# Giving every large SBUF slot of a transformer-block kernel a size that is a whole number of 256 bytes

## The chip, the cores and the metric

The kernel runs on one core of one Trainium2 chip. The metric is the device time of one execution in microseconds. The kernel before takes 2279.22 us (median of 3 runs, 2278.37 to 2279.22).

## What is computed

One layer of an encoder block on x, 1024 rows (T) of 1024 channels (D), all in float32:

```
x <- x + 1/2 * SwiGLU_1(RMSNorm(x))            (D_FF = 2816)
h  = RMSNorm(x);  [x_m | z_m | x_r | y_r] = h @ W_in
y_m = mLSTM head group (4 heads of 256 channels, causal)
y_r = RG-LRU channel group (4 block-diagonal gate groups of 256, conv of 4, scan)
x <- x + concat[RMSNorm(y_m), RMSNorm(y_r)] @ W_out
x <- x + 1/2 * SwiGLU_2(RMSNorm(x))
out = RMSNorm_final(x)
```

Nearly all the arithmetic is matrix products with 1024 rows: two feed-forward blocks (1024 to 2 x 2816 to 1024), the input projection (1024 to 4096), the output projection (2048 to 1024), and the attention-like products of the four mLSTM heads.

## The kernel before

**Products.** The channels lie on the 128 partitions, the rows of x along the free axis. A float32 operand is carried as two float32r parts, hi and lo, and a product is the sum of three passes, hi*hi + hi*lo + lo*hi (`PASSES`). So each step of 128 channels issues three matmuls, each with a weight load of 128x128 of its own and with 512 columns streamed. `project_half` (L275 to L280, matmul on L278) makes a 128x512 tile of an up or input projection: 24 matmuls, 8 steps of channels (k) by 3 passes. The stationary operand is `wu`, a weight tile with its hi part and, 4096 bytes on, its lo part; the streamed operand is `hT`. `products` (L284 to L299, matmul on L295) makes the down and output projections the same way, with `wu` stationary and a pair of hi and lo activations (`u8` in the feed-forward blocks, other tiles in the output projection) streamed.

**Stages.** `ffn` (L311) makes two tiles of the hidden layer (192 matmuls on L278), then the 96 matmuls on L295 that add two earlier ones to x, and so on, 11 times. Between the two feed-forward blocks lie the input projection with the RG-LRU group (gates on L522), the mLSTM group's set-up, the four heads (scores L799, values L828, transposes L867, with products of the output projection between them), and the rest of the output projection.

**Where operands lie.** Pools of tiles are laid end to end in each partition. The pool of raw weights (slots of 4096 bytes), `wup` (4 slots of 8192 bytes, L37) and `bigp` (6 slots, L38) come first; the slots of `wup` begin at 19296 + 8192 i, the first slot of `bigp` at 52064, in the built program. Both are 96 modulo 256. A slot of a pool is as large as the largest tile that it ever holds. `bigp` holds x, `hT` (`new_hT`, L193: four tiles of 16384 bytes, hi and lo for each half of the rows) and the values `v` of a head (L685), which has 2 x 8 x 258 elements and is the largest:

```
hd["v"] = bigp.tile([P, 2, NT, 258], R32, tag="big", name="v")
```

That is 16512 bytes, 64 x 256 + 128, so the six slots begin in turn at 96 and at 224 modulo 256. In what follows, the **offset** of a matmul is the start of its streamed operand minus the start of its stationary operand, modulo 256 bytes. Every step inside these tiles (2048, 4096 or 512 bytes) is a multiple of 256, so the offset depends on the two slots alone. By the addresses of the built program the 5760 matmuls on L278 have offset 0 in 2544 cases and 128 in 3216:

| block | half of the rows | hi part in a slot at | lo part in a slot at | offsets of the three passes |
|---|---|---|---|---|
| first feed-forward | 0 | 224 | 96 | 128, 0, 128 |
| first feed-forward | 1 | 96 | 224 | 0, 128, 0 |
| second feed-forward | 0 | 96 | 224 | 0, 128, 0 |
| second feed-forward | 1 | 224 | 224 | 128, 128, 128 |

The input projection has 0, 128, 0 in half 0 and 128, 0, 128 in half 1. The tiles `u8` of the feed-forward blocks lie at 96 modulo 256: all of their products have offset 0. The pools inside the mixer begin at 192 (`rg`, `xm`, `ml`, `wo`), behind small tiles of the pool `mix` (`bg` on L412, `gs` on L720 among them), so the RG-LRU gates (L522) have offset 96, and so do 96 of the matmuls on L295, while 192 more there have 128. Over the whole program 5679 of 10052 matmuls have offset 0. Behind `bigp` lie the pools of the stages, and from the other end of the partition the pool of the norm (`nrm`, L360), which holds `rb_late`, the factors of the rows of a late norm (L213), and `rb`, two buffers of 512 rows, for the other norms (L229, L260).

Of the kernel before, what the change touches and what calls it, by code (L numbers as in the profile page):

```python
# [8 lines left out]
F32 = mybir.dt.float32  # L9
R32 = mybir.dt.float32r  # L10
# [9 lines left out]
H = 4  # L20
EPS = 1e-6
NEG = -1e30
# a float32 operand is carried as two float32r parts, hi + lo; a product is hi*hi + hi*lo + lo*hi
PASSES = ((0, 0), (0, 1), (1, 0))
# [6 lines left out]
def hymba_block_kernel(ctx: ExitStack, tc, xT, chv, qkv, kblk, wgate, bgate, up1, dn1, up2, dn2,  # L31
# [33 lines left out]
    def half_of(h):  # L65
        return slice(h * 512, (h + 1) * 512)
# [10 lines left out]
    def open_psum(a, b):  # L77
        """a tiles of two banks and b of one; what was open before is closed."""
        for k in ("A", "B"):
            if k in psum:  # L80
                psum.pop(k + "ctx").__exit__(None, None, None)
                psum.pop(k)
        for k, n in (("B", b), ("A", a)):
            if n:
                psum[k + "ctx"] = tc.tile_pool(name=f"ps{k}", bufs=n, space=bass.MemoryType.PSUM,
                                               reuse_waits="tile")
                psum[k] = psum[k + "ctx"].__enter__()
# [7 lines left out]
    def t2(pool):  # L95
        return pool.tile([P, 512], F32, tag="t2", name="t2", bufs=4)
# [41 lines left out]
    def row_rstd(pool, rs_pool, acc, tag, bank=bank_b):  # L138
        """1/sqrt(mean over the channels + eps) of the rows, 128 rows to a column."""
        n = acc.shape[1] // P  # L140
        ps = bank()[:, 0:2 * n].rearrange("p (t o) -> p t o", o=2)
        for t in range(n):
            nc.tensor.matmul(ps[:, t], lhsT=acc[:, t * P:(t + 1) * P], rhs=ones[:, 0:2],  # L143
                             start=True, stop=True)
        ms = pool.tile([P, n], F32, tag="ms", name="ms", bufs=2)
        nc.vector.tensor_scalar(out=ms, in0=ps[:, :, 0], scalar1=1.0 / D, scalar2=EPS,
                                op0=ALU.mult, op1=ALU.add)
        rs = inv_sqrt(rs_pool, ms, tag)
        parts = rs_pool.tile([P, 2, n], R32, tag=tag + "p", name="parts", bufs=2)
        nc.vector.tensor_copy(parts[:, 0], rs)  # L150
        nc.vector.tensor_tensor(out=parts[:, 1], in0=rs, in1=parts[:, 0].bitcast(F32), op=ALU.subtract)
        return parts
# [25 lines left out]
    def defer(n, fn):  # L178
        """Issue fn after n further groups of products, so that they cover what it waits for."""
        waiting.append([n, fn])  # L180
# [16 lines left out]
    class Norm:  # L197
        """RMSNorm of x in halves of 512 rows, into hT or out; with late, hT holds x * gain and
        the factor of each row is left in rb."""

# [24 lines left out]
        def spread(self, xs, h, rs):  # L225
            if self.late:
                in_every_partition(lambda: t2(self.pool), rs, self.rb[:, half_of(h)])
                return
            rb = self.pool.tile([P, 512], F32, tag="rb", name="rb", bufs=2)  # L229
            in_every_partition(lambda: t2(self.pool), rs, rb)  # L230
            if self.hT is None:
                self.hT = new_hT()
            for m in range(NK):
                xn = t2(self.pool)
                nc.vector.scalar_tensor_tensor(out=xn, in0=row(xs, m)[:, half_of(h)],  # L235
                                               scalar=chan(self.gain, m), in1=rb,
                                               op0=ALU.mult, op1=ALU.mult)
                split(self.hT[0][h][:, m], self.hT[1][h][:, m], xn,
                      nc.gpsimd if m % 2 else nc.vector)

    class LastNorm:
        """RMSNorm of x in place, in pieces of the rows, which then leave for out."""

        def __init__(self, pool, gain, pieces):
            self.pool, self.gain, self.pieces, self.acc = pool, gain, pieces, [[] for _ in pieces]

        def feed(self, xs, m, i):
# [9 lines left out]
        def spread(self, xs, i, rs):  # L257
            sl = self.pieces[i]
            n = sl.stop - sl.start
            rb = self.pool.tile([P, 512], F32, tag="rb", name="rb", bufs=2)[:, 0:n]  # L260
            pb = in_every_partition(lambda: t2(self.pool), rs, rb)
            for m in range(0, NK, 2):
                xt = xs[m // 4][:, m % 4:m % 4 + 2, sl]
                nc.vector.tensor_tensor(out=xt[:, 0], in0=xt[:, 0], in1=pb, op=ALU.mult)
                eng, by = (nc.gpsimd, rb) if m < 6 else (nc.vector, pb)
                eng.tensor_tensor(out=xt[:, 1], in0=xt[:, 1], in1=by, op=ALU.mult)
                nc.sync.dma_start(out=out[m * P:(m + 2) * P, sl].rearrange("(c p) t -> p c t", p=P), in_=xt)
# [16 lines left out]
    def products(lhs, rhs, apply, half_major, pieces=halves, bank=bank_b):  # L284
        """rows of weights (stationary) times activations of the same channels, summed into x; one
        function for each tile of x."""
        order = [(m, h) for m in range(NK) for h in range(len(pieces))]
# [69 lines left out]

# [1 line left out]
    def norm_pool(name):  # L359
# [32 lines left out]

# [1 line left out]
    with tc.tile_pool(name="mix", bufs=1, reuse_waits="tile") as mix:  # L394
# [16 lines left out]
        nc.sync.dma_start(out=comp, in_=qkv)  # L411
        bg = mix.tile([P, 2 * H], F32, name="bg")  # L412
        nc.sync.dma_start(out=bg, in_=bgate.broadcast_to([P, 2 * H]))
# [15 lines left out]
        nc.vector.memset(tail[:, 0, :, 0:1], 1.0)  # L429
        # q k^T is xc (Wq Wk^T / 16) xc^T, and Wq Wk^T has the blocks of Wq and Wk  # L430
        kb = raw_tile()[:, 0:NK * 16].rearrange("p (c j o) -> p c j o", c=NK, j=4)
# [64 lines left out]
        with tc.tile_pool(name="rg", bufs=10, reuse_waits="tile") as pool:  # L496
            # RG-LRU channel group
            acc = pool.tile([P, T], F32, tag="accr", name="accr", bufs=1)
# [90 lines left out]
        with tc.tile_pool(name="xm", bufs=4, reuse_waits="tile") as pool:  # L589
            # gate weights composed with the block-diagonal maps  # L590
            wg = raw_tile()[:, 0:3 * NK * 8 * H].rearrange("p (w c o g) -> p w c o g", w=3, c=NK, o=4)
# [21 lines left out]
            def after_projection(c, xm, xp):  # L613
                """Values and gates of one group of channels, in two parts."""
                bd = block_diag_pair(pool, 1, c)
# [45 lines left out]
        def prepare(h, bank):  # L661
            """The pieces of work that set up a head of the mLSTM group."""
            hd = heads[h] = {}
# [19 lines left out]
            def values(j):  # L683
                if j == 0:
                    hd["v"] = bigp.tile([P, 2, NT, 258], R32, tag="big", name="v")  # L685
                    hd["negm"] = raw_tile()
                    nc.sync.dma_start(out=hd["negm"], in_=m_d[h:h + 1, :].broadcast_to([P, T]))
# [9 lines left out]

        # mLSTM head group
        with ExitStack() as ml:
# [8 lines left out]

            # log forget gates, their running sums and the running maxima, between the projections
            gr = spare()  # L710
# [4 lines left out]
            def gates_by_row():  # L715
                gp = bank_b()[:, 0:NT * 4 * H].rearrange("p (t g) -> p t g", t=NT)
                for t in range(NT):
                    nc.tensor.transpose(out=gp[:, t], in_=gr[0:4 * H, t * P:(t + 1) * P],
                                        identity=ident[0:4 * H, 0:4 * H])
                gs = mix.tile([P, NT, 4 * H], F32, name="gs")  # L720
                nc.vector.tensor_copy(gs, gp)
# [64 lines left out]

            # products of w_out after each step, and the groups of products that cover the last head's
            # output, its norm and the rows that follow from it
            FEED = (2, 1)
# [27 lines left out]
            def attend(h, ih, J, pc, st):  # L817
# [6 lines left out]
                for I in range(max(J, 4 * ih), 4 * ih + 4):  # L824
                    u = I - 4 * ih
                    js = [j for j in ORDER[ih] if j <= I]
                    for n, (a, b) in enumerate(PASSES):
                        nc.tensor.matmul(st["av"][u][:, 0:258], lhsT=pc[:, a, u * P:(u + 1) * P],  # L828
                                         rhs=v[:, b, J], start=(J == js[0] and n == 0),
                                         stop=(J == js[-1] and n == 2))  # L830
# [126 lines left out]

            # the output projection starts with the RG-LRU channels: its products lie between the
            # heads, where those of a head would have to wait for the other engines
            between = []  # L960
# [85 lines left out]

# [1 line left out]
    with tc.tile_pool(name="f2", bufs=4, reuse_waits="tile") as pool:  # L1048
# [66 lines left out]
```

## Time and profile before

| | |
|---|---|
| median of 3 runs | 2279.22 us (2278.37 to 2279.22) |
| span of the profiled execution | 2279.1 us |
| TensorE matmul busy | 2235.8 us, 98% of the span, 10102 matmuls |
| weight loads (overlap the matmuls) | 1820.6 us, 80% |
| VectorE / ScalarE / GpSimd busy | 1112.5 / 663.0 / 363.6 us |
| DMA | 152.13 MB, mean 67 GB/s |
| mean granted TensorE clock | 0.995 |

The span is one profiled execution's own time, from the first to the last instruction; it lies 0.1 us under the median of the runs. TensorE is the engine to read: it is busy nearly throughout, and the chain of work that ended last is 87% TensorE. Matmuls are pipelined: one is recorded from its start to the end of its results, so the record of a 512-column matmul is about 390 ns long while the next one starts some 230 ns after it. In a stretch without waits, the time per matmul is the length of the stretch over the number of matmuls, and a record that is longer by so many ns goes with a later start of the next by as many.

### The profile page before, as it was taken

The page shows a single profiled execution, that of the slowest core. Times are in us where ns is not written, and L with a number is a line of the kernel's source. Part 1 is how long each engine was busy: PE and PEld are TensorE (multiplying, and loading weights), DVE is VectorE, ACT ScalarE, POOL GpSimd, SP SyncE. Part 2 cuts the span into 40 slices and gives each one's busy share as a digit, 9 for nine tenths or more (in the row PEclk, how much of TensorE's full clock was granted, in tenths as well). Part 3 has the DMA queues.
Part 4 walks back from the last instruction along what each step waited for, and adds up shares of the span by engine and source line. Part 5 has one row for each costly group of instructions (what it writes and reads, how often), then busy time and mean ns, then how long its engine had stood idle before and what let it go on. Part 6 is the DMA issues. An engine that isn't in the chain of part 4 may idle for free.

```text
span 2279.1 us, 24258 instructions
## 1 busy us (share of the span) xinstructions
PE 2235.8 (98%) x10102; PEld 1820.6 (80%) x10102; DVE 1112.5 (49%) x1567; ACT 663.0 (29%) x865; POOL 363.6 (16%) x217
## 2 busy tenths in 40 slices
PE   8999999999999999999999999989999999999998
PEld 5888888888888788877778887768888888888887
DVE  6333343333443645665538998872333333333334
ACT  5111111111112445555545553241111111111114
POOL 3000000000002301232311113431000000000004
PEclk9999999999999999999999999999999999999999
DMA  4111111111112311122256322201111111111102
GB/s 172 52 47 47 47 47 45 48 56 47 47 56 71 116 37 65 63 102 84 83 170 200 102 65 83 75 27 48 47 37 56 47 52 51 47 47 37 56 19 74
DMA packets 62070, 152.13 MB, mean 67 GB/s; under 512 B 5380, under 2 KB 24068, under 8 KB 60936
## 3 DMA queue, kind: packets, MB, share of 16 engines
q1 hardware_dynamic: 61960, 150.58, 19.7%
q8 instruction: 79, 1.29, 0.2%
q14 instruction: 31, 0.25, 0.0%
HBM read 124.85 MB, written 25.71 MB: 66 GB/s over the span
## 4 chain that ended last, share of the span: by engine, by line
PE 87%; DVE 8%; issue 2%; POOL 1%; ACT 1%; DMA 0%; SPq 0%; POOLq 0%; DVEq 0%; ACTq 0%
PE bank_a L278 55%; PE bank_b L295 23%; PE bank_s L295 3%; PE bank_a L522 2%; DVE xs L953 1%; PE bank_b L828 1%; DVE wu L103 1%; PE bank_s L799 1%; DVE hT L107 1%; DVE t L235 1%; DVE w L943 1%; POOL r L135 1%; PE bank_b L625 0%; DVE w L812 0%; PE bank_b L143 0%
## 5 line engine op out<-in xcount | busy, mean ns | idle before, releaser
L278 PE MATMUL bank_a<-hT,wu 128*128 128x512 f32 x5712 | 1342.3, 395 | 12.6 <-ACT wu L102 6.1
L278 PEld LDWEIGHTS bank_a<-hT,wu 128*128 128x128 f32 x5712 | 1073.2, 188 | 269.0 <-DVE hT L107 7.7
L295 PE MATMUL bank_b<-u,wu 128*128 128x512 f32 (+1 forms) x2496 | 556.9, 383 | 2.4 <-DVE xs L338 1.4
L295 PEld LDWEIGHTS bank_b<-u,wu 128*128 128x128 f32 x2496 | 456.7, 189 | 97.9 <-DVE xs L953 3.0
L102 ACT CAST wu<-raw 128x1024 fp32r<-128x1024 f32 (+1 forms) x183 | 188.2, 1043 | 1141.7 <-PE bank_a L278 564.8
L338 DVE SCALAR_TENSOR_TENSOR xs<-bank_b,xs 128x512 f32<-128x512 f32 (+1 forms) x328 | 220.0, 676 | 179.5 <-PE bank_b L295 177.2
L325 POOL TENSOR_TENSOR t<-t,rb_late 128x1024 f32<-128x1024 f32 x44 | 105.4, 2397 | 1224.3 <-ACT t L324 1224.3
L103 DVE TENSOR_TENSOR wu<-raw,wu 128x1024 fp32r<-128x1024 f32 (+1 forms) x183 | 226.4, 1246 | 59.1 <-ACT wu L102 59.1
L327 DVE TENSOR_TENSOR t<-t,bank_a 128x1024 f32<-128x1024 f32 x44 | 53.8, 1222 | 377.3 <-PE bank_a L278 373.7
L323 DVE TENSOR_TENSOR t<-rb_late,bank_a 128x1024 f32<-128x1024 f32 x44 | 53.7, 1221 | 322.1 <-PE bank_a L278 319.7
L295 PE MATMUL bank_s<-wu 128*128 128x512 f32 x384 | 98.6, 397 | 3.3 <-ACT wu L102 2.4
L488 DVE SCALAR_TENSOR_TENSOR t<-bank_a,ch,t 128x1023 f32<-128x1023 f32 (+2 forms) x48 | 61.4, 1278 | 49.1 <-ACT t L485 48.5
L295 PEld LDWEIGHTS bank_s<-wu 128*128 128x128 f32 x384 | 69.5, 188 | 19.4 <-ACT wu L102 3.5
L174 POOL TENSOR_TENSOR acc<-acc,t 128x512 f32<-128x512 f32 (+1 forms) x47 | 62.0, 1319 | 113.0 <-ACT t L172 61.9
L102 ACT CAST u<-t 128x1024 fp32r<-128x1024 f32 (+1 forms) x56 | 57.3, 1022 | 26.4 <-DVE t L327 13.7
L799 PE MATMUL bank_s<-q,k 128*128 128x512 f32 (+3 forms) x288 | 61.3, 347 | 0.9 <-DVE q L103 0.6
L828 PE MATMUL bank_b<-v,pc 128*128 128x258 f32 x432 | 61.8, 287 | 0.0
L828 PEld LDWEIGHTS bank_b<-v,pc 128*128 128x128 f32 x432 | 58.9, 192 | 2.7
L799 PEld LDWEIGHTS bank_s<-q,k 128*128 128x128 f32 x288 | 48.1, 190 | 7.9 <-DVE q L103 1.0
L103 DVE TENSOR_TENSOR u<-t,u 128x1024 fp32r<-128x1024 f32 x44 | 53.7, 1221 | 1.1 <-ACT u L102 1.1
L953 DVE TENSOR_TENSOR xs<-xs,bank_b 128x512 f32<-128x512 f32 x64 | 42.8, 681 | 17.1 <-PE bank_b L295 16.9
L324 ACT ACTIVATE t<-t 128x1024 f32<-128x1024 f32 x44 | 46.7, 1062 | 7.8 <-DVE t L323 7.8
(207 smaller groups left out, 1368.9 us busy)
## 6 DMA issues: line engine op xcount, KB each, us to landing
raw<-in_up_dram SPq DMA_DIRECT2D x87, 512.0 KB, 3.5
raw<-in_dn_dram SPq DMA_DIRECT2D x44, 512.0 KB, 3.5
raw<-in_win_dram SPq DMA_DIRECT2D x32, 512.0 KB, 3.5
v_d<-u SPq DMA_DIRECT2D x8, 1024.0 KB, 3.8
v<-v_d SPq DMA_DIRECT2D x16, 512.0 KB, 6.7
raw<-in_wout_dram SPq DMA_DIRECT2D x16, 512.0 KB, 3.7
xs<-in_xT_dram SPq DMA_DIRECT2D x16, 256.0 KB, 6.0
x_d<-xs SPq DMA_DIRECT2D x16, 256.0 KB, 2.0
```

Source lines behind the costliest of these rows:

```text
L102: nc.scalar.copy(hi, src)
L103: (eng or nc.vector).tensor_tensor(out=lo, in0=src, in1=hi.bitcast(F32), op=ALU.subtract)
L174: eng.tensor_tensor(out=box[0], in0=box[0], in1=sq, op=ALU.add)
L278: nc.tensor.matmul(ps, lhsT=w[:, a, k * P:(k + 1) * P], rhs=hT[b][half][:, k], start=(k == 0 and n == 0), stop=(k == NK - 1 and n == 2))
L295: nc.tensor.matmul(ps, lhsT=w[:, a, m * P:(m + 1) * P], rhs=u[:, b, pieces[h]], start=(i == 0 and n == 0), stop=(i == len(lhs) - 1 and n = ...
L325: nc.gpsimd.tensor_tensor(out=s, in0=s, in1=rb, op=ALU.mult)
L327: nc.vector.tensor_tensor(out=s, in0=s, in1=pu, op=ALU.mult)
L338: nc.vector.scalar_tensor_tensor(out=xt, in0=ps, scalar=0.5, in1=xt, op0=ALU.mult, op1=ALU.add)
L488: nc.vector.scalar_tensor_tensor(out=y[:, s:], in0=ps[:, :T - s], scalar=chan(f"{name}c{3 - s}", c), in1=y[:, s:], op0=ALU.mult, op1=ALU.add)
L799: nc.tensor.matmul(s[:, o:], lhsT=hd["k"][:, j, a, J * P:(J + 1) * P], rhs=hd["q"][:, j, b, ih * 512 + o:(ih + 1) * 512], start=(j == 0 an ...
L828: nc.tensor.matmul(st["av"][u][:, 0:258], lhsT=pc[:, a, u * P:(u + 1) * P], rhs=v[:, b, J], start=(J == js[0] and n == 0), stop=(J == js[- ...
L953: nc.vector.tensor_tensor(out=xt, in0=xt, in1=ps, op=ALU.add)
```

## The change

The largest tile of `bigp`, `v`, gets rows of 260 elements instead of 258 (`VW`), of which the matmuls still read 258. Its slot is then 16640 bytes, 65 x 256, and all six slots begin at 96 modulo 256. In the pool `mix`, `bg` is padded by 160 bytes and `gs` (512 bytes) moves into a spare tile of the pool `ml`, so that the pools of the mixer begin at 96 modulo 256 as well. For the room, the two `rb` buffers of a norm go: `Norm` and `LastNorm` use slices of one tile in the slot of `rb_late`. Comments and docstrings are taken out, which moves line numbers.

```diff
+VW = 260
...
-            rb = self.pool.tile([P, 512], F32, tag="rb", name="rb", bufs=2)
-            in_every_partition(lambda: t2(self.pool), rs, rb)
             if self.hT is None:
                 self.hT = new_hT()
+                self.rb = self.pool.tile([P, T], F32, tag="rb_late", name="rb", bufs=1)
+            rb = self.rb[:, half_of(h)]
+            in_every_partition(lambda: t2(self.pool), rs, rb)
...
+            self.rb = None
...
-            rb = self.pool.tile([P, 512], F32, tag="rb", name="rb", bufs=2)[:, 0:n]
+            if self.rb is None:
+                self.rb = self.pool.tile([P, T], F32, tag="rb_late", name="rb", bufs=1)
+            rb = self.rb[:, sl]
...
-        bg = mix.tile([P, 2 * H], F32, name="bg")
+        bg = mix.tile([P, 2 * H + 40], F32, name="bg")[:, 0:2 * H]
...
-                    hd["v"] = bigp.tile([P, 2, NT, 258], R32, tag="big", name="v")
+                    hd["v"] = bigp.tile([P, 2, NT, VW], R32, tag="big", name="v")
...
-                gs = mix.tile([P, NT, 4 * H], F32, name="gs")
+                gs = spare()[:, 0:NT * 4 * H].rearrange("p (t g) -> p t g", t=NT)
...
-                                         rhs=v[:, b, J], start=(J == js[0] and n == 0),
+                                         rhs=v[:, b, J, 0:258], start=(J == js[0] and n == 0),
```

In the built program of the change 9340 of 10052 matmuls have offset 0. Of those on L278 all but 96 have it: these 96 take their weights from a tile at 224 in the pool of the norm, for the first block of the input projection and of the second feed-forward block each. All on L522 and all on L295 have it, and so do the scores on L799, which had it before.

Every engine issues the same instructions in the same order. Waits differ in a handful of places, and two are new there. One is on GpSimd in the RG-LRU stage (a step of `rg_scans`, L542) and is for a product of the first feed-forward block, since its tile now reaches into bytes that `u8` had. The other is on VectorE, where the gates are turned into columns of rows (`gates_by_row`, L715) between the last blocks of the input projection; `t` are values of a group of channels, `gt` the gates, `k` the keys of the first head. Before:

```order
435 L629 TENSOR_TENSOR t_7025<-t_7025,bank_b 128x256 [waits DVE_49,Activation_49]
436 L629 TENSOR_TENSOR t_7025<-t_7025,bank_b 128x256 [waits Activation_49] x3
437 L721 COPY gs<-bank_b 128x128 [waits PE_49]
438 L722 TENSOR_TENSOR gt<-gs 128x64 [waits DVE_49]
439 L103 TENSOR_TENSOR k<-xc,k 128x1024 [waits DMAHW3_49,DMAHW4_49,DMAHW1_49,Activation_49]
440 L723 TENSOR_TENSOR gt<-gt,bg 128x64 [waits DVE_49]
```

And now:

```order
435 L638 TENSOR_TENSOR t_7024<-t_7024,bank_b 128x256 [waits DVE_49,Activation_49]
436 L638 TENSOR_TENSOR t_7024<-t_7024,bank_b 128x256 [waits Activation_49] x3
437 L730 COPY pc<-bank_b 128x128 [waits DMAHW7_49,PE_49,Pool_49]
438 L731 TENSOR_TENSOR gt<-pc 128x64 [waits DVE_49]
439 L106 TENSOR_TENSOR k<-xc,k 128x1024 [waits DMAHW3_49,DMAHW4_49,DMAHW1_49,Activation_49]
440 L732 TENSOR_TENSOR gt<-gt,bg 128x64 [waits DVE_49]
```

The copy out of PSUM now goes into a tile `pc`, over bytes that the stage before used, and so it also waits for GpSimd's last but one split of values and for the store of that tile to `v_d` (the seventh of the eight stores on L632).

## Rows read from the trace of the kernel before

**Rows 1.** The page, busy time of each engine and its share of the span:

```profile
PE 2235.8 (98%) x10102; PEld 1820.6 (80%) x10102; DVE 1112.5 (49%) x1567; ACT 663.0 (29%) x865; POOL 363.6 (16%) x217
```

**Rows 2.** Chain of work that ended last, first feed-forward block: start us, us, what

```profile
42.37 65.47 PE bank_a L278 x283
107.85 21.78 PE bank_b L295 x96
129.63 44.41 PE bank_a L278 x192
```

**Rows 3.** The chain, input projection with the RG-LRU gates:

```profile
834.98 11.20 PE bank_a L522 x48
846.18 44.43 PE bank_a L278 x192
```

**Rows 4.** The chain, end of the output projection, and second feed-forward block:

```profile
1464.34 36.67 PE bank_b L295 x156
...
1621.50 21.81 PE bank_b L295 x96
1643.31 44.56 PE bank_a L278 x192
```

**Rows 5.** Whole run by line and shape: count, busy us, mean ns, idle before, releasers:

```profile
L278 PE MATMUL bank_a<-hT,wu 128*128 128x512 f32 x5712 | 1342.3, 395 | 12.6 <-ACT wu L102 6.1 <-DVE hT L107 3.6 <-ACT t L550 1.1
...
L295 PE MATMUL bank_s<-wu 128*128 128x512 f32 x384 | 98.6, 397 | 3.3 <-ACT wu L102 2.4 <-DVE wu L103 0.8
L828 PE MATMUL bank_b<-v,pc 128*128 128x258 f32 x432 | 61.8, 287 | 0.0
```

**Rows 6.** By line, 307.3 to 328.1 us, down products of the first block:

```profile
L295 PE MATMUL bank_b<-u,wu 128*128 128x512 f32 x93 | 21.2, 389 | 0.0
```

**Rows 7.** By line, 295.2 to 300.6 us, half 0 of a projection, first block:

```profile
L278 PE MATMUL bank_a<-hT,wu 128*128 128x512 f32 x25 | 5.9, 392 | 0.0
```

**Rows 8.** By line, 300.7 to 306.2 us, half 1 of the same projection:

```profile
L278 PE MATMUL bank_a<-hT,wu 128*128 128x512 f32 x25 | 6.0, 394 | 0.0
```

**Rows 9.** By line, 1643.4 to 1648.8 us, half 0 of a projection, second block:

```profile
L278 PE MATMUL bank_a<-hT,wu 128*128 128x512 f32 x25 | 5.9, 391 | 0.0
```

**Rows 10.** By line, 1649.0 to 1654.4 us, half 1 of that projection:

```profile
L278 PE MATMUL bank_a<-hT,wu 128*128 128x512 f32 x25 | 6.0, 395 | 0.0
```

**Rows 11.** By line, 1301.5 to 1304.1 us, output products between the heads:

```profile
L295 PE MATMUL bank_s<-wu 128*128 128x512 f32 x12 | 2.9, 392 | 0.0
```

**Rows 12.** By line, 1311.1 to 1312.2 us, the same products a little later:

```profile
L295 PE MATMUL bank_s<-wu 128*128 128x512 f32 x7 | 1.8, 389 | 0.0
```

**Rows 13.** Matmuls on v (L828): duration ns min/median/max, first and last start:

```profile
L828 PE MATMUL bank_b<-v,pc x432: 277/282/419, 1201.0 to 1407.0; 128*128 128x258 f32 x144
```

**Rows 14.** Timeline about the copy of the gates: SyncE's store, GpSimd, then VectorE:

```profile
1145.39 0.32 SPq L632 DMA_DIRECT2D v_d<-u  x1
...
1142.96 2.40 POOL L103 TENSOR_TENSOR u<-t,u 128x1024 fp32r<-128x1024 f32 x1 [3.24 <-ACT u L102]
...
1165.16 0.29 DVE L721 COPY gs<-bank_b 128x128 f32<-128x128 f32 x1 [9.44 <-PE bank_b L718]
```

**Rows 15.** Stores on L632, landing after issue, us min/median/max:

```profile
DMA to landing us min/median/max: 3.8/3.8/4.7
```

**Rows 16.** Windows, first block: length, busy us PE, PEld, DVE, ACT, POOL; PEclk; DMA:

```profile
63.50:107.80 44.30, 44.30 (x193) 35.95 (x192) 11.94 (x10) 8.35 (x8) 4.86 (x2) 1.00 0.15 48
107.90:129.60 21.70, 21.70 (x97) 17.96 (x96) 13.59 (x18) 2.68 (x3) 0.00 (x0) 1.00 0.08 25
```

## The prediction, made before the changed kernel ran

> **What bounds the kernel now.** I read the page first. TensorE is busy for 2235.8 of 2279.1 us [rows 1], so time can only go if matmuls become fewer or follow each other faster. Their number stays. So the next question is what one matmul costs, and the chain of waits answers it, because it has long stretches without a wait. In the first feed-forward block 96 down products take 21.78 us and the 192 matmuls of two tiles of the hidden layer 44.41 us [rows 2]: 226.9 ns and 231.3 ns each. Both stream 512 columns, both load 128x128 weights, both ran at a granted clock of 1.00 [rows 16], which is the upper level, 2.4 GHz. At that level 512 columns are 213.3 ns; so 14 ns of a down product and 18 ns of a projection are something else. In the second block the same division gives 227.2 and 232.1 ns [rows 4], in the input projection 231.4 and for the RG-LRU gates 233.3 [rows 3], and for the output projection's last units 235.1 [rows 4].
>
> What tells these stretches apart is the offset between the two operands. The down products have offset 0 throughout: about 227. The gates have 96 throughout, the last output units 128 and 96: 233 to 235. The projections on L278 mix 0 and 128: 231 to 232. VectorE is no explanation: it is busier beside the down products, 13.59 of 21.7 us, than beside the projections, 11.94 of 44.3 [rows 16], and they are the faster ones.
>
> The record of one matmul says the same at a finer grain: 389 ns for the down products [rows 6], and within the projections of the second block 391 in half 0, where two passes of three have offset 0, and 395 in half 1, where none has [rows 9, 10].
>
> **The change, part by part.**
>
> *The projections on L278.* 5664 of 5760 get offset 0; I take the 226.9 ns of the down products [rows 2] for each, because it is the only long run of offset 0 in the trace.
> - First block: 2112 matmuls, but until 42 us TensorE waits for x and weights, and what is saved there is waited for instead. The chain has 283 in its first long piece [rows 2], and nine more pairs of tiles of 192, together 2011, follow: 2011 x (231.3 - 226.9) = 8.9 us.
> - Input projection: 32 blocks of 48, less the one whose weights stay at 224: 1488 x (231.4 - 226.9) = 6.7 us [rows 2, 3].
> - Second block: 2112 - 48 = 2064 x (232.1 - 226.9) = 10.7 us [rows 2, 4].
>
> *RG-LRU gates, L522.* 192 x (233.3 - 226.9) = 1.2 us [rows 2, 3].
>
> *Output projection, last units.* 288 matmuls on L295 go from 128 or 96 to 0. By the chain 288 x (235.1 - 226.9) = 2.4 us [rows 2, 4], but that piece has pauses in it; by the gates' 233.3, which has none, 1.8. I take 1.8.
>
> *Settling.* Offset 0 alone does not give 389 ns at once. Between the heads the output products have offset 0 too, and there the records are 392 ns in one stretch and 389 in a later one [rows 11, 12], where more of them stand in a row; over all 384 of them the mean is 397 with waits and shorter neighbours [rows 5]. So after each interruption some matmuls are still slow. The feed-forward blocks will have almost none, since projections and products then form one run. In the mixer the projections are cut by small matmuls, by an estimate from the code some sixty times (eight blocks with eight groups of values and gates); 6 matmuls by 3 ns (392 less 389) each time are 1.1 us. I take 1.0 off.
>
> *The matmuls on v, L828.* Their streamed operand steps by 1040 bytes instead of 1032. Before, such a matmul is 277 ns at least and 282 in the median [rows 13], 287 in the mean [rows 5], at sixteen different offsets. Bounds: all 432 at the least, a gain of 432 x 10 = 4.3 us; as much lost, if the steps of 16 find the worse ones. I take 0, since the mean lies near the median, and put 4.3 on both ends.
>
> *Waits.* The copy of the gates now waits for a store issued at 1145.39 us, which lands 4.7 us later at most, and for a split that ended at 1145.36; it started at 1165.16 [rows 14, 15]. It costs 0, with 15 us of cover. Should the store be later than the copy, the splits of k behind it on VectorE, and so the first head's maps, would be late. The new wait on GpSimd is for a product of the first block, done before the input projection began: 0. The rows' factors in one tile instead of two buffers: every instruction that writes or reads them waits for the same as before: 0. The padding of `bg` and the spare tile for `gs` add no instruction.
>
> Sum: 8.9 + 6.7 + 10.7 + 1.2 + 1.8 - 1.0 = 28.3 us. Can the other engines follow? VectorE has 49% [rows 1], and the matmul groups' own idle time is small, 12.6 us before all of L278 [rows 5]; a TensorE that is 2% faster in these stages meets nobody who is full. From the span, 2279.1 - 28.3 = 2250.8 us; the median of the runs is 0.1 above the span, so 2251 us.
>
> **Rivals.**
>
> *A. Offset is not what matters* (or the two read streams do not meet), and the down products are faster for another reason: two weight tiles instead of one, or another PSUM tile. For: the difference between projections and products is also one of code. Against: gates, output units and half 1 of the second block's projections have constant offsets other than 0 and are all slow (233.3 ns, 235.1 ns, records of 395), whichever code issues them. Time: 2279 us, within the L828 bounds.
> The Trainium skill, page "TensorE: Matmul & The Clock Gate", section "Step-by-step: what each phase is for", says that loading the next tile's weights takes no SBUF read bandwidth from the running matmul, because each has a read port of its own; by that rule no offset could matter and the sum would be 0. The rows speak against it: 389 against 395 ns at one clock with weight loads beside both [rows 6, 10].
>
> *B. Offset 0, but it never settles in the projections.* Their streamed operand alternates between two slots, hi and lo, which the products' does not, and the trace has no long run of that kind with offset 0. Then they stay where the output products between the heads are, 392 ns [rows 11], 3 above the settled 389: 226.9 + 3 = 229.9 ns. Saved: 5563 x about 1.8, and 192 x 3.4 for the gates, 11 us: 2268 us.
>
> *C. Slower.* In the first block the half with two passes of three at offset 0 has 394 ns and the half with one of three 392 [rows 7, 8]. If offset 0 is what is dear in a projection, 2 ns for a third, all three give 396, about 3 ns above the 393 between the halves: 5563 x 3 = 17 us, 2296 us. What decides is whether the cost hangs on the offset or on its changing from pass to pass: both halves change twice in three. Against C: in the second block the order is the other way, 391 with two of three and 395 with none [rows 9, 10].
>
> **How the numbers follow.** The forecast, offset 0 settling at about 227 ns in all three stages, gets 0.79: three kinds of constant offset in one trace and only 0 is fast. B gets 0.11, A 0.06, C 0.04. A measurement of this kernel can tell some 0.2%, 4.6 us, from no change. The forecast and B are faster by more than that: 0.90. A is the same: 0.06. C is slower: 0.04. The forecast's own range is 2246 to 2257: the L828 bound of 4.3 below; above, the same and a settling twice as long. With 2 in 10 left out at most, the range reaches half-way into B, where only some stages settle: 2246 to 2263.
>
> **What would show each step.** Right: the chain's pieces of 192 on L278 at 43.6 us instead of 44.4 in both blocks and the input projection; records of L278 at 389 ns in both halves of a projection; gates at 10.9 us for 48; the pieces of 96 products unchanged. The idle time before TensorE's groups stays near 43 us in all. Wrong: L278 at 392 (B), at 393 to 395 (A), or at 396 and more (C); a VectorE wait for a DMA at the copy of the gates; or a saving on L278 that comes back as idle time before it, with VectorE or ScalarE as the releaser.

## The result, and the profile after

The changed kernel takes 2248.98 us (median of 4 runs, 2247.87 to 2249.78) where the kernel before, now with a fourth run, takes 2279.09 us (2278.37 to 2279.22): a ratio of 0.9868, 95% interval 0.9854 to 0.9882. It is 30.1 us faster; the forecast was 28 us less, 2251 us, with a range of 2246 to 2263. Line numbers of the changed kernel are 7 to 9 higher at the matmuls: L278 is now L285, L295 L302, L522 L531, L828 L837, L721 L730.

The page of the changed kernel's profile, busy time of each engine (against [rows 1]):

```profile
PE 2202.3 (98%) x10102; PEld 1816.0 (81%) x10102; DVE 1110.4 (49%) x1567; ACT 663.4 (30%) x865; POOL 365.2 (16%) x217
```

TensorE has the same 10102 matmuls and 33.5 us less busy time; the other engines stay within 2.1 us of what they had. The span of this execution is 2246.5 us, so TensorE idles 44.2 us, against 43.3 before: hardly anything came back as waits.

Now the chain of work that ended last in the changed kernel, from start to end (start us, us, what): the first feed-forward block, the input projection with the gates, the output projection's last units, and the second block (against [rows 2, 3, 4]):

```profile
42.23 64.17 PE bank_a L285 x283
106.40 21.76 PE bank_b L302 x96
128.16 43.52 PE bank_a L285 x192
...
824.30 10.88 PE bank_a L531 x48
835.18 43.52 PE bank_a L285 x192
...
1447.38 35.68 PE bank_b L302 x156
...
1598.89 21.76 PE bank_b L302 x96
1620.65 43.52 PE bank_a L285 x192
```

Every piece of 192 is 43.52 us, in all three stages, where they were 44.41, 44.43 and 44.56. The pieces of 192 projections, of 96 products and of 48 gates now all divide to the same 226.7 ns per matmul. The down products, which had offset 0 before, hardly moved (21.78 and 21.81 to 21.76).

By line and shape, the four halves of projections that correspond to [rows 7 to 10] (count, busy us, mean ns, idle before). They lie at 258.9 to 264.0, 264.3 to 269.5, 1620.8 to 1626.0 and 1626.2 to 1631.5 us, and all four read alike, so one stands here:

```profile
L285 PE MATMUL bank_a<-hT,wu 128*128 128x512 f32 x25 | 5.8, 389 | 0.0
```

392, 394, 391 and 395 ns have become 389, the record of the settled products in [rows 6]. What was particular to a half is gone with the difference in offset. The six slots are 65 x 256 bytes long, so that they begin in turn at 96 and at 352 modulo 512; projections from all of them are alike, so 256 bytes, and not more, is the length after which the offset starts anew.

### The profile page after: what moved, and what is told of

Read it like the earlier page. It is cut to its first block, busy times and chain, and to the rows that moved or that the text cites. A ratio compares the mean times of both kernels' runs of the same rounds, so it can differ in the third digit from the quotient of the medians.

```text
span 2246.5 us, 24257 instructions
## 1 busy us (share of the span) xinstructions
PE 2202.3 (98%) x10102; PEld 1816.0 (81%) x10102; DVE 1110.4 (49%) x1567; ACT 663.4 (30%) x865; POOL 365.2 (16%) x217
## 4 chain that ended last, share of the span: by engine, by line
PE 86%; DVE 7%; issue 2%; POOL 2%; ACT 1%; DMA 0%; SPq 0%; POOLq 0%; DVEq 0%; ACTq 0%
PE bank_a L285 54%; PE bank_b L302 23%; PE bank_s L302 3%; PE bank_a L531 2%; PE bank_s L808 1%; PE bank_b L837 1%; DVE wu L106 1%; DVE xs L962 1%; DVE hT L110 1%; DVE t L239 1%; DVE w L952 1%; POOL r L138 1%; PE bank_b L634 0%; PE bank_b L619 0%; PE bank_b L616 0%
## 5 line engine op out<-in xcount | busy, mean ns | idle before, releaser
L285 PE MATMUL bank_a<-hT,wu 128*128 128x512 f32 x5712 | 1313.3, 390 | 14.6 <-ACT wu L105 6.2
L285 PEld LDWEIGHTS bank_a<-hT,wu 128*128 128x128 f32 x5712 | 1070.3, 188 | 245.1 <-DVE hT L110 8.1
L302 PE MATMUL bank_b<-u,wu 128*128 128x512 f32 (+1 forms) x2496 | 555.2, 382 | 2.5 <-DVE xs L345 1.3
L302 PEld LDWEIGHTS bank_b<-u,wu 128*128 128x128 f32 x2496 | 456.9, 189 | 95.8 <-DVE xs L962 3.3
L302 PE MATMUL bank_s<-wu 128*128 128x512 f32 x384 | 97.9, 396 | 3.1 <-ACT wu L105 2.3
L302 PEld LDWEIGHTS bank_s<-wu 128*128 128x128 f32 x384 | 69.5, 188 | 18.6 <-ACT wu L105 3.2
L837 PE MATMUL bank_b<-v,pc 128*128 128x258 f32 x432 | 61.0, 284 | 0.0
L837 PEld LDWEIGHTS bank_b<-v,pc 128*128 128x128 f32 x432 | 58.0, 190 | 2.7
```

Source lines behind the costliest of these rows:

```text
L285: nc.tensor.matmul(ps, lhsT=w[:, a, k * P:(k + 1) * P], rhs=hT[b][half][:, k], start=(k == 0 and n == 0), stop=(k == NK - 1 and n == 2))
L302: nc.tensor.matmul(ps, lhsT=w[:, a, m * P:(m + 1) * P], rhs=u[:, b, pieces[h]], start=(i == 0 and n == 0), stop=(i == len(lhs) - 1 and n = ...
```

## Experiments

All theories speak of what one 512-column matmul costs in a long run: 226.7 ns when good, 229 to 237 otherwise. It is read from the chain, as the length of a piece over its count. Each kernel has line numbers of its own; the tile names are the same. Each theory has a name in capitals, which the expectations explain. OFFSET is the forecast's: the cost is set by the offset.

### Only the big slots, only the mixer, and all addresses moved by 160 bytes

Three kernels, each one line away from the changed one. In slots_only the mixer's pools go back to 192 modulo 256:

```diff
-        bg = mix.tile([P, 2 * H + 40], F32, name="bg")[:, 0:2 * H]
+        bg = mix.tile([P, 2 * H + 0], F32, name="bg")[:, 0:2 * H]
```

In mixer_only the big slots have 16512 bytes again:

```diff
-VW = 260
+VW = 258
```

In abs_shift all pools that are laid from the front of the partition lie 160 bytes further on:

```diff
-    ch = const.tile([P, len(CHANNEL) * NK], F32, name="ch")
+    ch = const.tile([P, len(CHANNEL) * NK + 40], F32, name="ch")[:, 0:len(CHANNEL) * NK]
```

> The change with the pools of the mixer at 192 modulo 256 as before, so that only the six big slots are moved. Theory OFFSET (what a matmul costs is set by the start of the streamed operand minus that of the stationary one, modulo 256 bytes): the projections stay at 226.7 ns (192 in 43.5 us) in both feed-forward blocks and the input projection; the RG-LRU gates go back to 233 ns (48 in 11.2 us) and the last units of the output projection to 44 to 47 us for 192, so the time is some 2 us above the changed kernel's 2249, about 2251 us. Theory ADDRESS (what counts is where the streamed operand itself begins, 96 modulo 256 being good): the same here. Theory STEADY (the loss came from the offset changing from pass to pass; any constant offset is good): the projections at 226.7 ns, and the gates too, since their offset of 96 is constant.

> The change with rows of 258 in v, so that the big slots lie at 96 and 224 as before and only the pools of the mixer are moved. OFFSET and ADDRESS: projections at 231 to 232 ns as before (192 in 44.4 us), gates at 226.7 ns (48 in 10.9 us), 2 us less than before in all, about 2277 us. STEADY: the same projections, since their passes change offset again; gates as before.

> The changed kernel with 160 bytes more in front of all pools, so that the weights, the big slots and the pools of the mixer begin at 0 modulo 256 instead of 96, all offsets 0 as in the changed kernel. OFFSET and STEADY: no change, 226.7 ns for the projections and products, about 2249 us. ADDRESS: the projections and products leave 226.7 ns, in either direction (230 ns or more, or nearer to the 213.3 ns of 512 columns); each ns is 8.7 us, so 2220 or 2278 us.

Measured, against the same kernel before (2279.59 us, the median of 13 runs beside these): slots_only 2252.59 us, ratio 0.9884 (0.9869 to 0.9898); mixer_only 2275.43 us, 0.998 (0.9971 to 0.999); abs_shift 2247.89 us, 0.9863 (0.9848 to 0.9877). The chains, gates and projections of the input projection, of slots_only:

```profile
826.24 11.21 PE bank_a L531 x48
...
892.23 43.56 PE bank_a L285 x192
```

of mixer_only, with a piece of the second block:

```profile
834.81 10.92 PE bank_a L531 x48
845.73 44.31 PE bank_a L285 x192
...
1635.14 44.56 PE bank_a L285 x192
```

and of abs_shift:

```profile
824.50 10.88 PE bank_a L531 x48
...
835.38 43.52 PE bank_a L285 x192
```

The two parts add up: 27.0 us from the big slots and 4.2 from the mixer, 31.2 in all, where the whole change gave 30.1. For the mixer alone I had expected 2 us; by the interval of its ratio it is 2.3 to 6.6, and the gates and the last output units, of which the expectation names the gates alone, are worth 3.1 by their pieces (1.3 and 1.8). Each part moves its own matmuls, and others hardly: with the mixer put back, the gates are at 233.5 ns again and the projections stay at 226.7 to 226.9; with the slots put back, the gates are at 227.5 and the projections at 230.8 and 232.1. The gates in slots_only have a constant offset of 96 and are slow, so theory STEADY falls. In abs_shift these operands lie at 0 modulo 256 instead of 96, and the pieces of 192, 96 and 48 are as long as in the changed kernel to 0.01 us: theory ADDRESS falls. What counts is where operands lie to each other. One of my numbers for slots_only was loose: of the last output units only 96 leave offset 0 there, and most of the long piece of 156 lies ahead of them, so that it hardly moves (35.68 to 35.85 us), and 44 to 47 us for 192 was never at stake.

### Other constant offsets

Five kernels with gaps between pools, so that each kind of product has a constant offset of its own. The first, as an example (32 floats are 128 bytes; the others differ in the numbers; for offsets that are no multiple of 32 bytes the tiles `u8` are made 256 bytes longer and begun a few floats in):

```diff
+    gap = ctx.enter_context(tc.tile_pool(name="gap", bufs=1))
+    gap.tile([P, 32], F32, name="gap")
     bigp = ctx.enter_context(tc.tile_pool(name="bigp", bufs=6))
...
+        pool.tile([P, 40], F32, name="gap1", bufs=1)
         norm = Norm(nrm, "n1", True)
...
-        bg = mix.tile([P, 2 * H + 40], F32, name="bg")[:, 0:2 * H]
+        bg = mix.tile([P, 2 * H + 48], F32, name="bg")[:, 0:2 * H]
...
+        pool.tile([P, 48], F32, name="gap2", bufs=1)
         norm_out = LastNorm(
```

> The changed kernel with gaps between pools: constant offsets of 128 for all projections on the big slots, 32 for the down products of the first feed-forward block, 64 for those of the second, 160 for the RG-LRU gates. OFFSET: 128 gives 233 to 234 ns (192 in 44.8 us, as half 1 of the second block before), 32 and 64 and 160 lie between 226.7 and 236 ns, and the time is about 2249 + 5664 x 7 ns = 2289 us plus some 2000 x 0 to 7 ns, 2289 to 2303 us. STEADY: all of them at 226.7 ns, 2249 us. ADDRESS: as OFFSET for the projections (224 modulo 256 is then bad); it says nothing else.

> As offs_a with other constant offsets: 64 for the projections on the big slots, 160 for the down products of the first feed-forward block, 192 for those of the second, 32 for the RG-LRU gates. OFFSET, with the value of an offset the same wherever it stands: projections at 229 ns (what the products had with 64 in offs_a), products of the first block at 234 ns (what the gates had with 160), gates at 233 ns (what the products had with 32), 192 not yet seen, 226.7 to 236; time 2249 + 5664 x 2.3 + about 2000 x 3 to 7 ns + 192 x 7 ns, 2269 to 2278 us. Theory KIND (the offset that is good differs with the code, since hi and lo of the projections lie in two tiles): projections with 64 elsewhere than 229 ns by more than 2 ns.

> As offs_a with 224 for the projections, 96 for the products of the first block, 128 for those of the second, 192 for the gates. OFFSET: products of the first block at 233 ns (what the gates had with 96 before), of the second at 232 to 234 ns (what the projections had with 128), 224 and 192 not yet seen but above 226.7 ns, and if 224 counts as 32 the wrong way round, near 233; time 2249 + 5664 x 6.5 + 2000 x 6.5 ns, about 2299 us. A theory in which only a streamed operand that begins behind its weights is slowed would have 224 (32 before them) at 226.7 ns, and about 2262 us.

> Finer offsets: 16 bytes for the down products of the first block, 4 for those of the second; 192 for the projections and 224 for the gates. Theory WINDOW (offset 0 is good because the two reads then meet the same 32 bytes or so at the same time; a few bytes more don't matter): 4 and 16 stay at 226.7 ns. Theory EXACT (0 alone is good): 4 and 16 at 230 ns or more. Projections with 192 between 226.7 and 234, gates with 224 as the projections in offs_c.

> The last offsets: 240 (16 before the weights) for the products of the first block, 252 (4 before) for those of the second, 160 for the projections and 128 for the gates. OFFSET, EXACT: projections at 234.3 ns (what products and gates had with 160), gates at 233 ns (as projections and products with 128), 240 and 252 above 228 ns. If the sign of a small offset matters (4 behind gave 236.6, 16 behind 231.7), 252 or 240 may come to 226.7 or under it, and would then be a better place for all operands than 0: 2240 us or less. Time else 2249 + 5664 x 7.6 + 2000 x 5 to 10 + 2 = 2304 to 2314 us.

Times, one run each: 2294.71, 2277.78, 2302.21, 2301.66 and 2299.22 us, beside 2279.59 to 2280.14 for the kernel before. Four of the five are slower than before; offs_b cannot be told from it by one run. Where a time was expected, offs_a and offs_b lie inside it, offs_c 3 us over it and offs_e 5 us under its range; with 252 as good as 0, the terms of offs_e still add up to about 2304 us, so its miss is not explained. From the chains, in each kernel projections and products of the first block, then products of the second; offs_a (128, 32, 64), with projections of the second block too:

```profile
130.87 44.80 PE bank_a L287 x192
175.67 22.40 PE bank_b L304 x96
...
1633.06 21.99 PE bank_b L304 x96
1655.05 44.62 PE bank_a L287 x192
```

offs_b (64, 160, 192):

```profile
129.73 43.95 PE bank_a L287 x192
173.67 22.50 PE bank_b L304 x96
...
1618.02 22.39 PE bank_b L304 x96
```

offs_c (224, 96, 128):

```profile
131.37 44.80 PE bank_a L287 x192
176.17 22.41 PE bank_b L304 x96
...
1635.16 22.40 PE bank_b L304 x96
```

offs_d (192, 16, 4):

```profile
130.39 44.79 PE bank_a L292 x192
175.18 22.24 PE bank_b L309 x96
...
1631.21 22.72 PE bank_b L309 x96
```

and offs_e (160, 240, 252):

```profile
131.60 44.98 PE bank_a L292 x192
176.58 22.71 PE bank_b L309 x96
...
1636.64 21.77 PE bank_b L309 x96
```

Divided by the counts, with the gates' first three pieces (48 matmuls each, not shown) and the kernel before for what they add:

| offset, bytes | products, ns | projections, ns | gates, ns |
|---|---|---|---|
| 0 | 226.7 | 226.7 | 226.7 |
| 4 | 236.7 | | |
| 16 | 231.7 | | |
| 32 | 233.3 | | 233.3 |
| 64 | 229.1 | 228.9 | |
| 96 | 233.4 | | 233.3 (before) |
| 128 | 233.3 | 233.3, in the second block 232.4 | 232.1 to 232.7 |
| 160 | 234.4 | 234.3 | 234.2 |
| 192 | 233.2 | 233.3 | 233.3 |
| 224 | | 233.3 | 233.3 |
| 240 | 236.6 | | |
| 252 | 226.8 | | |

Theory OFFSET holds: the same offset costs the same within 1.2 ns wherever it stands, in products with one streamed slot and in projections with two. The widest case is 128: in offs_a the projections, all with offset 128, take 44.80 us in the first block and 44.62 in the second, in one execution. By the starts in the trace the intervals follow two different patterns there (229 or 230 and 237 or 238 ns in turn; then 241, 232, 231, 232, 228, 230, 232 over and over, or nearly), so the offset alone leaves a little of the cost open. Theory KIND falls. So does the theory that only a stream behind its weights is slowed: 224 and 240, before them, are slow. EXACT falls with 252, four bytes before, which is as good as 0; WINDOW, in the form I gave it, falls too, since 4 bytes behind is as bad as any. No piece goes below 226.7 ns.

### Whose weights?

A matmul's weights are loaded while the one before it streams: in the trace of the changed kernel a weight load begins 3 ns after a matmul has started and is 188 ns long, and the load beside the last matmul of one line of code already has the next line. Two kernels ask whether the offset that counts is to its own weights or to the weights that are loaded while it streams, the next matmul's. In `lo_both` the lo parts begin 32 bytes late; in `pair_shift` the second of the two weight tiles of a down product and its activations do, by 32 and by 128 bytes. Both give a buffer of the heads (`w`, three to two) for the room. The core of lo_both, where `d` is 8 floats for `wu`, and 0 or 8 for the `u8` of the first or second block:

```diff
+            self.p = (t[:, 0:T], t[:, T + d:2 * T + d])
...
+        lo = [bigp.tile([P, NK * 512 + 64], R32, tag="big", name="hT") for _ in range(2)]
+        return [hi, [t[:, 8:8 + NK * 512].rearrange("p (k n) -> p k n", k=NK) for t in lo]]
```

The core of pair_shift, where `later` is 8 floats in the first block and 32 in the second:

```diff
-            rows = [weights(dn[f]) for f in fs]
+            rows = [weights(dn[f], d=later[0] * (f % 2)) for f in fs]
...
-                gt = pair(pool, "u8")
+                gt = pair(pool, "u8", later[0] * (f % 2))
```

> Which weights does a streamed operand meet, its own or the next matmul's, which are loaded while it runs? Here the lo parts of the weights and of the projections' streamed operand both begin 32 bytes later than the hi parts. With the passes hi-hi, hi-lo, lo-hi the offset of a streamed operand to its own weights is then 0, 32, 224, but to the weights of the next matmul 0, 0, 0. The down products of the first block keep their streamed operand in place, so that their offsets to the next weights are 0, 224, 0, and to their own 0, 0, 224; those of the second block are displaced like the projections. Theory NEXT (what runs into each other is the stream of a matmul and the load of the next one's weights): projections, and products of the second block, at 226.7 ns, products of the first block above 228. Theory OWN (the offset to the own weights): projections and products of the second block at 229 to 234 ns, products of the first block also above 228. In both the mixer may be a little slower, since one of its buffers is taken for the room.

> lo_both kept every stream at offset 0 to the weights loaded while it runs, and was slow; so NEXT alone is out. Here the down products take their two weight tiles in turn, three matmuls each, and the second weight tile and its activations both begin later than the first, by 32 bytes in the first block and by 128 in the second. The offset of every stream to its own weights is 0; to the next matmul's weights it is 0, 0, and at the change of tile 32 or 128 off. Theory OWN (the own weights alone): products of both blocks settle at 226.7 ns (96 in 21.8 us), time about 2249 us. Theory ALL (streams and weight loads must all begin alike, as each meets what goes before and behind it): products at 229 to 234 ns in both blocks (96 in 22.0 to 22.5 us), and 2000 x 2 to 7 ns more time, 2253 to 2263 us. In both, the projections stay at 226.7 ns.

Measured: lo_both 2296.24 us, pair_shift 2260.51 us, one run each, beside 2280.09 and 2280.14. The chain of lo_both, projection, products of the first block (streams in place) and of the second:

```profile
131.24 44.59 PE bank_a L297 x192
175.83 22.39 PE bank_b L314 x96
...
1631.50 22.29 PE bank_b L314 x96
```

and of pair_shift, products of the first block, a projection, and products of the second:

```profile
172.91 22.27 PE bank_b L309 x96
195.18 43.55 PE bank_a L292 x192
...
1738.94 22.08 PE bank_b L309 x96
```

In lo_both all streams of projections are at 0 to the weights loaded beside them, and still cost 232.2 ns: NEXT alone falls. In pair_shift all streams of products are at 0 to their own weights, and cost 232.0 and 230.0 ns: OWN alone falls. ALL was expected to give 229 to 234 ns and 2253 to 2263 us, and did. In these runs 226.7 ns was reached only where the streams and loads of a whole run begin alike (or, with 252, all streams 4 bytes ahead). That all of them have to is not shown: a matmul may need both pairings at once, or its own weights and the stream before it, and no kernel here tells these apart.

## Why the prediction was right

**The terms.** By the pieces of the chain: the first block saves 1.30 us in its long piece and nine times 0.89, 9.3 us (forecast 8.9); the input projection 1488/192 x 0.91 = 7.1 (6.7); the second block 2064/192 x 1.04 = 11.2 (10.7); the gates 4 x 0.32 = 1.3 (1.2); the last output units 288/156 x 0.99 = 1.8 (1.8). Together 30.7 against 29.3, mostly because I took 226.9 ns for a good matmul, the mean of a product piece that still had to settle at its start (by the starts in the trace 235, 229, 232, 231 ns, then 226 or 227); settled it is 226.7, and 5563 x 0.2 is 1.1 us.

**Settling.** In the changed kernel 5418 of 5653 intervals behind projections of offset 0 without a wait are 226 or 227 ns, by the starts in the trace. The others, with those over 300 ns left aside, cost 1.6 us more than that in all, 1.3 of it between the feed-forward blocks, where I had taken 1.0. That it came so near is luck, since two errors went against each other: other matmuls break the projections there 28 times, not sixty, and each break costs 46 ns in the mean, not 6 times 3. 30.7 less 1.3 is 29.4 us of the 30.1 between the runs.

**The base.** I added 0.1 us to go from the span to the median of the runs. That compared two executions: in the runs here the time lies about 1.7 us above the span of the same execution (2248.25 against 2246.5 us), so the profiled execution before was about 1.6 us slower than the three runs. The 2251 us are none the worse for it, since 2279.2 less 28.3 is 2250.9. But the two profiled spans differ by 32.6 us, 2.5 more than the runs, and those two executions also differ in mean granted clock, 0.995 and 0.997; so I go by the runs.

**What I put at nothing.** The matmuls on v, by duration (min, median, max; against [rows 13]), and the copy of the gates with its new wait, in the timeline of VectorE (against [rows 14]):

```profile
L837 PE MATMUL bank_b<-v,pc x432: 276/282/368, 1185.2 to 1390.0; 128*128 128x258 f32 x144
```

```profile
1149.76 0.29 DVE L730 COPY pc<-bank_b 128x128 f32<-128x128 f32 x1 [9.31 <-PE bank_b L727]
```

The median on v is the same 282 ns; by line their mean is 284 ns against 287 [rows 5] and their busy time 61.0 us against 61.8, so at most 0.8 us came from here. The copy is still released by TensorE last, and takes 0.29 us as before. The engines that work on the rows' factors `rb` idle 4.7 us until ScalarE has written them, as before.

**The rivals.** A, that offset is not what matters, falls with the table: one kernel, with its tiles moved by gaps, ranges from 2249 to 2302 us. By the Trainium skill, page "TensorE: Matmul & The Clock Gate", section "Step-by-step: what each phase is for", a weight load takes no read bandwidth from the running matmul. By that rule it should not matter how the two lie to each other; the trace does not agree, with 226.7 ns at offset 0 and 236.7 at 4. B, that the projections would not settle because hi and lo lie in two slots, falls with 389 ns in all four halves. C, that offset 0 is what is dear in a projection, falls with the same 389, where it gave 396. What C rested on, two passes of three at offset 0 being dearer than one in the first block (394 against 392 ns [rows 7, 8]), stays open: the passes 0, 128, 0 cost 394 ns there and 391 in the second block [rows 8, 9], so the offsets of a mixed run alone do not give its cost. I was right to doubt that a run of mixed offsets tells what a run of equal ones costs.

**What was argued and not shown.** I wrote of two read streams that meet. The runs show that the relation of addresses sets the interval, not what in the chip does so: neither pairing of a stream with a load explains it alone. This is open. That a faster TensorE would meet no other engine that is full was right; its idle time rose by 0.9 us.

## What to carry to other kernels

Where TensorE is the bound and a weight load goes with every matmul, as here, look at the start addresses of both operands modulo 256 bytes: here a whole run at equal starts is 3% quicker per 512-column float32r matmul than one at 32 to 224 bytes apart (64 aside, which costs 1%), and six slots that were 128 bytes over a multiple cost 1.2% of the kernel. The place to see it is the length of a wait-free piece of the chain over its count, compared between lines with the same shape. Two quotients that differ by a few ns are not noise when every piece of their kind in the trace has the same length: before, nine pieces of projections in the first block were 44.41 us each. A tail of a few elements in one rarely used tile can set the slot size, and with it the start modulo 256, of every other tile in its pool.

## What the runs showed that I had not expected

The curve is not smooth: four bytes behind the weights cost 236.7 ns, as much as any, and four before them 226.8, as good as none. 16 before costs 236.6 and 16 behind 231.7; 64 lies a third of the way from good to bad (229 ns).

The good interval is a state that a run falls into. Between the heads the same products at offset 0 have records of 392 ns in one stretch and of 389 in a later one [rows 11, 12]. Behind an interruption the starts in the trace follow each other after 234, 235, 225, 230, 236, 229, 232 and 231 ns, then after 226 or 227; the projections of the changed kernel at 1139.7 us go through the same numbers as the output products of the kernel before at 1301.5 us.

At the lower granted clock, 0.50, which is 1.2 GHz, offset costs nothing that the trace shows. In one stretch behind waits for VectorE the output products follow each other after 427 ns, with offset 96 in the kernel before (1517.1 to 1520.4 us) and with offset 0 in the changed one (1497.6 to 1501.4 us). By an estimate from this, half the time at twice the clock, the same 512 columns would take some 213.3 ns at 2.4 GHz. Every good run ends at 226.7, 13.4 above that, and none of the offsets tried came under it.
